# A two-layer encoder on one core: another order for the first stage's loads and products, and half a projection moved ahead of the second pair's gates

## The chip, the cores and the metric

The kernel runs on one core of a Trainium2 chip. The metric is the device time of one execution in microseconds. Engines are named as the profile names them: PE multiplies matrices (PEld loads its weights), DVE, ACT and POOL work on vectors, SP issues the DMAs.

## The reference

A hybrid encoder with two layers, 1024 tokens of 1024 channels, in float32. Cut to what matters:

```python
def even_mixer(h, ...):                       # layer 0
    q, k, v, g_a, x_b, g_b = split(h @ w_in)
    a_out = diff_attention(q, k, v, ...)      # 4 heads, two softmax maps each, RMS norm per head
    xc = depthwise_conv(x_b, conv_w) + conv_b
    gate_a, gate_x = sigmoid(xc @ w_a + b_a), sigmoid(xc @ w_x + b_x)   # per direction
    log_a = -LRU_C * gate_a * softplus(-lam)
    u = sqrt(-expm1(2 * log_a)) * gate_x * xc
    b_out = scan(exp(log_a), u) + reverse_scan(exp(log_a), u)
    return concat(a_out * silu(g_a), b_out * silu(g_b)) @ w_out

def odd_mixer(h, ...):                        # layer 1: 16 heads over an 8 x 16 window
    q, k, v, g = split(h @ w_in)
    return (neighborhood_attention(q, k, v, rpb) * silu(g)) @ w_out

for l in range(2):
    shift, scale, gate = split(silu(c) @ ada_w[l] + ada_b[l])
    h = rms_norm(x, norm_g[l]) * (1 + scale) + shift
    x = x + gate * (even_mixer, odd_mixer)[l](h)
return rms_norm(x, final_g)
```

## The kernel before

Everything is kept transposed, channels on the partitions, tokens along the row, in two halves of 512 tokens (half 0 and half 1). A weight slab is 128 output columns of a weight matrix. To keep float32 accuracy each operand is split into a high and a low part: ACT writes a slab's high part (`whi`, L189), POOL its low part in four pieces (`wlo`, L192), and each 128x128 by 128x512 product is three matmuls: high by high, low activations, low weights (L208 to L210, and L577 to L579 in the first stage). A projection of one slab for one half is eight products, 24 matmuls into one PSUM bank. The activations' parts are `ahi` (ACT, L419) and `alo` (DVE, L420).

A scheduler places instructions by priority, in the order of the code; `tc.issue_after(x)` holds what follows behind x, `tc.high_priority()` lets it go ahead. Each engine then runs its instructions in that fixed order, and so do the DMA queues, which SP fills in the order in which it issues.

**The first stage** (L517 to L624) loads x in 16 pieces `xT` and squares them (`sq`), sums the squares over the channels on PE (`norm`), makes 1/sqrt on DVE by Newton steps (`rstd_rows`, L385), and spreads it back with PE (`spread`). `mod_first(g)` loads eight pieces of the modulation's weights (`ada`), sums on PE (`mod`, 32 small matmuls) and gives the scale and shift of channel blocks 2g and 2g+1. `parts(g, hf)` scales those blocks of a half into `ahi` and `alo`, and `products(i, g, hf)` multiplies them with slab i of the first three. Slabs 0 and 1 hold x_b, from which the convolution starts (ACT L715, DVE L723, then the parts `xch` and `xcl` for the gates).

**The recurrent part.** A list of jobs sets PE's order: projections, and `pair(c, c+1)`, which makes the gates (`gate`) of two channel blocks, then their exponentials and square roots on ACT (table loads between), then the input factors (L795), the two scans (L798, L800) and their sum (L802) on DVE. The names of the projections are `gb` (the branch gate g_b, whose PSUM bank is read last by DVE at L681, `sgb`), `v3` (the fourth block of v), and `k0`, `q0` (keys and queries of head 0). There are four PSUM banks for projections, given out in turn: `k0` of half 1 takes the bank that `gb2` of half 1 has left, and can't start before DVE's L681 on it.

**The layer boundary.** The last block of layer 0's output is added to x (DVE L1153), squared (ACT L1158), added to the running sum (DVE L1164) and summed on PE (`ssl`). Behind it PE starts layer 1's projections.

**rstd_rows** is called twice in the first stage, for eight head norms in layer 0's attention (`osq`, then `obc` on PE and `vT` on DVE), and at the boundary.

Of the kernel before, what the change touches and what calls it, by code (L numbers as in the profile page):

```python
# [15 lines left out]
ALU = mybir.AluOpType  # L16
# [81 lines left out]
def kernel(ctx, tc, xT, xTp, small, lamp, adaw, tb, w0, gw, wo0, w1, nab, wo1, out):  # L98
# [53 lines left out]
    def load_next():  # L152
        i = state["load"]
        if i >= len(slabs):
            state["load"] = i + 1
            return
        raws[i] = wp.tile([P, KC, P], F32, tag="raw", name=f"raw{i}")
        nc.sync.dma_start(raws[i][:], slabs[i])
        state["load"] = i + 1

    def split_next():
        i = state["split"]
        if i >= len(slabs):
# [20 lines left out]
        hi = pool.tile([P, KC, P], F32R, tag=tags[0], name=f"whi{i}")  # L184
        lo = pool.tile([P, KC, P], F32R, tag=tags[1], name=f"wlo{i}")

        with (tc.issue_after(state["tanh"]) if i == at1["k", 1] else nullcontext()), (
                tc.high_priority() if j < 2 else tc.issue_after(state["pool"])):
            A.activation(hi[:], raw[:], AF.Copy)  # L189

            for k in range(0, KC, 2):
                G.tensor_tensor(lo[:, k:k + 2], raw[:, k:k + 2], hi[:, k:k + 2], ALU.subtract)  # L192
        ready[i] = (hi, lo)
        state["split"] = i + 1
        while state["load"] <= i + state["depth"]:
            load_next()
# [80 lines left out]

    def mod_first(g, pool, small, c32):

        ps = ptp.tile([P, HF], F32, tag="pt", name=f"mod{g}")  # L280

        def sums(x, w, start, stop):
# [6 lines left out]
        for k in range(KC):  # L289
# [4 lines left out]
            src = adaw[0, k * P:(k + 1) * P, :2 * D].rearrange("p (t n) -> p t n", t=2)  # L294
            state["ada"] = nc.sync.dma_start(piece[:], src[:, :, 2 * g * P:(2 * g + 2) * P])
            pieces.append(piece)
        if g == 0:
            for k in range(KC):
                sums(pieces[k], c32[:, k, :], k == 0, k == KC - 1)
# [85 lines left out]
    def rstd_rows(ss, n, pool, spare=None, add=EPS):  # L385


        if spare is not None:
            v, rr, t = (spare[:, i * P:(i + 1) * P] for i in range(3))
        else:  # L390
            v, rr, t = (pool.tile([P, P], F32, tag=g, name=g)[:] for g in ("rs", "rr", "rt"))
        V.tensor_scalar(v, ss[:, :P], 1.0 / n, add, ALU.mult, ALU.add)
        V.tensor_scalar(rr.bitcast(I32), v.bitcast(I32), -0.5, float(0x5F3759DF),
                        ALU.mult, ALU.add)
        for _ in range(3):
            V.scalar_tensor_tensor(t, rr, -0.5, rr, ALU.mult, ALU.mult)
            V.tensor_tensor(t, t, v, ALU.mult)
            V.scalar_tensor_tensor(rr, t, 1.5, rr, ALU.add, ALU.mult)
        return rr

    def rstd_rows_act(ss, n, pool, w):
# [6 lines left out]

    def spread(rr, bc, w=P):
        for j in range(4):  # L410
            T.matmul(bc[:, j * w:(j + 1) * w], state["sel"][:, j, :], rr[:, :w], start=True, stop=True)

    def make_h(l, k, hf, x, bc):

# [17 lines left out]
    def evac_v(h):  # L432
# [3 lines left out]
            A.activation(mixed[h][:, hf * HF:(hf + 1) * HF], ps[:], AF.Copy)  # L436
        return f


    c_q, c_k, c_v, c_g, c_xb, c_gb = 0, 4, 8, 12, 16, 20  # L440
    order0 = [c_xb, c_xb + 1, c_v, c_xb + 2, c_xb + 3, c_v + 1, c_v + 2, c_gb, c_gb + 1]
    order0 += [c_v + 3, c_gb + 2, c_gb + 3, c_k, c_q]
    for h in range(1, DA_HEADS):
        order0 += [c_k + h, c_q + h]
    order0 += [c_g]
# [71 lines left out]
    with tc.tile_pool(name="start", bufs=2) as stp, tc.tile_pool(name="ada0", bufs=KC) as adp:  # L517
# [12 lines left out]
        def squares(hf, on_dve, pool, tag):  # L530
# [5 lines left out]
            for k in range(KC):  # L536
# [8 lines left out]
            if hf:  # L545
                ss_add(ss, sqs[KC - 1], True, False)
                with tc.issue_after(state["ssmm"].ins):
                    for k in range(KC - 1):
                        ss_add(ss, sqs[k], False, k == KC - 2)
# [17 lines left out]
        def products(i, g, hf):  # L567
# [7 lines left out]
            for k in (2 * g, 2 * g + 1):  # L575
                ps, (wh, wl), (hi, lo) = banks[i, hf], ready[i], hact[k, hf]
                T.matmul(ps, wh[:, k, :], hi[:], start=k == 0, stop=False)  # L577
                T.matmul(ps, wl[:, k, :], hi[:], start=False, stop=False)
                T.matmul(ps, wh[:, k, :], lo[:], start=False, stop=k == KC - 1)  # L579

        squares(0, (2, 5), pp, "pp")
        mod_first(0, adp, stp, c32)
        slab(0)
        scale(0)
        parts(0, 0)
        with tc.issue_after(state["ada"].ins):
            squares(1, (1, 4, 7), ptp, "pt")
        slab(1)
        with tc.issue_after(state["x"].ins):
            mod_first(1, adp, stp, c32)  # L590
        products(0, 0, 0)
        products(1, 0, 0)
        slab(2)
        with tc.issue_after(state["modmm"].ins):
            scale(1)
        parts(0, 1)
        with tc.issue_after(state["x"].ins):
            mod_first(2, adp, stp, c32)
        for i in range(2):
            products(i, 0, 1)  # L600

        rest = [(2, 0, 0), (2, 0, 1)]
        for g in range(1, KC // 2):
            if g == 1:
                with tc.issue_after(state["x"].ins):
                    mod_first(3, adp, stp, c32)
# [5 lines left out]
            for args in rest:  # L612
                products(*args)
            rest = [(2, g, 0), (2, g, 1)]
        for i, evac in enumerate((evac_xb(0), evac_xb(1))):
            for hf in range(2):
                evac(hf, banks[i, hf])
# [73 lines left out]
    def some(gen, n):  # L691
        for _ in range(n):
            next(gen, None)

    def after_dve(gen, n):

# [8 lines left out]
    with tc.tile_pool(name="lru", bufs=1) as lp:  # L705
# [178 lines left out]
        def mod_step():  # L884
            for m in parts_:
# [244 lines left out]
    def out_layer(l, ato, xsrc, xdst, pool, korder, order, view, segments):  # L1130
# [5 lines left out]
        def run(s):  # L1136
# [11 lines left out]
            for c in range(KC):  # L1148
                load(c + 1)

                def evac(hf_, ps, c=c):
# [463 lines left out]
```

## Time and profile before

| | |
|---|---|
| median of 3 runs | 1177.58 us (1175.38 to 1177.91) |
| profiled execution | 1177.39 us |
| its span | 1175.70 us (1.69 us lie outside it) |
| PE busy | 1141.5 us, 97% of the span |
| DVE, ACT, POOL busy | 715.5, 561.6, 442.4 us |

The span begins with the first instruction of the profile and all positions below are microseconds from there. A matmul's end is modelled: rows of 128x512 matmuls that follow each other start 0.23 us apart while each is given 0.39 us, so an idle time of PE in a row is 0.16 us shorter than what the wait really took from the next start.

### The profile page before, as it was taken

The page shows a single profiled execution, that of the slowest core. Times are in us where ns is not written, and L with a number is a line of the kernel's source. Part 1 is how long each engine was busy: PE and PEld are TensorE (multiplying, and loading weights), DVE is VectorE, ACT ScalarE, POOL GpSimd, SP SyncE. Part 2 cuts the span into 40 slices and gives each one's busy share as a digit, 9 for nine tenths or more (in the row PEclk, how much of TensorE's full clock was granted, in tenths as well). Part 3 has the DMA queues.
Part 4 walks back from the last instruction along what each step waited for, and adds up shares of the span by engine and source line. Part 5 has one row for each costly group of instructions (what it writes and reads, how often), then busy time and mean ns, then how long its engine had stood idle before and what let it go on. Part 6 is the DMA issues. An engine that isn't in the chain of part 4 may idle for free.

```text
span 1175.7 us, 19488 instructions
## 1 busy us (share of the span) xinstructions
PE 1141.5 (97%) x7232; PEld 972.5 (83%) x7232; DVE 715.5 (61%) x1420; ACT 561.6 (48%) x1032; POOL 442.4 (38%) x588
## 2 busy tenths in 40 slices
PE   5999999999999999999999999999999999999996
PEld 3788778888887888778879889988988998888896
DVE  6857968699899989768472434234444443454353
ACT  4357685476555556433343444344444444355221
POOL 3135445243333332466533433333243333417200
PEclk9999999999999999999999999999999999999998
DMA  9723141422122112485513533243453543314312
GB/s 330 241 71 118 54 141 54 143 85 80 32 82 79 32 38 73 144 301 183 179 60 117 153 104 101 87 141 113 119 160 98 156 147 96 95 35 154 101 73 72
DMA packets 85727, 136.48 MB, mean 116 GB/s; under 512 B 7936, under 2 KB 49408, under 8 KB 85632
## 3 DMA queue, kind: packets, MB, share of 16 engines
q1 hardware_dynamic: 85632, 135.23, 36.7%
q8 instruction: 57, 0.93, 0.3%
q14 instruction: 38, 0.31, 0.1%
HBM read 112.13 MB, written 16.78 MB: 110 GB/s over the span
## 4 chain that ended last, share of the span: by engine, by line
PE 79%; DVE 10%; ACT 5%; DMA 2%; POOL 2%; issue 1%; SPq 0%; DVEq 0%; ACTq 0%; POOLq 0%
PE pp L208 15%; PE pp L209 15%; PE pp L210 15%; PE no L1423 4%; PE etr L1405 3%; PE v L208 3%; PE v L210 3%; PE v L209 3%; PE n L675 2%; PE atr L1037 2%; DVE e L1007 2%; PE n L676 2%; POOL wlo L192 2%; PE s L675 2%; PE s L676 1%; DMA raw<-in_wo_dram 1%
## 5 line engine op out<-in xcount | busy, mean ns | idle before, releaser
L208 PE MATMUL pp<-ahi,whi 128*128 128x512 f32 (+1 forms) x976 | 370.0, 379 | 0.1
L209 PE MATMUL pp<-alo,whi 128*128 128x512 f32 (+1 forms) x976 | 368.1, 377 | 0.0
L210 PE MATMUL pp<-ahi,wlo 128*128 128x512 f32 (+1 forms) x976 | 367.6, 377 | 0.2 <-POOL wlo L192 0.2
L192 POOL TENSOR_TENSOR wlo<-raw,whi 128x256 fp32r<-128x256 f32 x320 | 265.6, 862 | 219.5 <-ACT whi L189 199.0
L210 PEld LDWEIGHTS pp<-ahi,wlo 128*128 128x128 f32 x976 | 183.8, 188 | 34.4 <-POOL wlo L192 0.6
L208 PEld LDWEIGHTS pp<-ahi,whi 128*128 128x128 f32 x976 | 183.8, 188 | 32.5 <-issue 1.1
L209 PEld LDWEIGHTS pp<-alo,whi 128*128 128x128 f32 x976 | 183.9, 188 | 30.6 <-issue 0.2
L1394 POOL TENSOR_SCALAR e<-e,r 128x288 f32<-128x288 f32 (+1 forms) x128 | 71.5, 572 | 221.0 <-DVE r L1392 215.7
L189 ACT ACTIVATE whi<-raw 128x1024 fp32r<-128x1024 f32 x80 | 84.4, 1057 | 106.2 <-PE pp L209 58.7
L1011 ACT ACTIVATE e<-e,nm 128x1024 f32<-128x1024 f32 x64 | 73.7, 1151 | 46.5 <-DVE nm L1007 46.2
L1389 ACT ACTIVATE e<-e,nm 128x288 f32<-128x288 f32 (+1 forms) x128 | 72.8, 570 | 46.4 <-DVE nm L1386 45.9
L1386 DVE CUSTOM_DVE_ANT_0 e<-n,bias 128x288 f32<-128x288 f32 (+1 forms) x128 | 60.6, 504 | 49.4 <-PE n L676 32.0
L1411 DVE COPY e<-etr 96x384 f32<-96x384 f32 (+1 forms) x64 | 35.5, 554 | 89.1 <-PE etr L1405 88.8
L1409 ACT ACTIVATE e<-etr 96x384 f32<-96x384 f32 (+1 forms) x64 | 31.4, 490 | 115.8 <-DVE e L1411 113.3
L1007 DVE CUSTOM_DVE_ANT_0 e<-s,tb 128x1024 f32<-128x1024 f32 x64 | 77.3, 1219 | 5.8 <-PE s L676 4.9
L1028 POOL TENSOR_SCALAR e<-e,r 128x256 f32<-128x256 f32 x32 | 32.7, 1021 | 124.4 <-DVE r L1017 75.7
L208 PE MATMUL v<-whi,ahi 128*128 128x256 f32 x256 | 72.2, 282 | 0.0
L210 PE MATMUL v<-whi,alo 128*128 128x256 f32 x256 | 71.9, 281 | 0.0
L209 PE MATMUL v<-wlo,ahi 128*128 128x256 f32 x256 | 71.9, 281 | 0.0
L1044 ACT ACTIVATE ath<-atr 128x512 fp32r<-128x512 f32 x64 | 37.5, 597 | 37.5 <-PE atr L1037 37.3
L1153 DVE SCALAR_TENSOR_TENSOR xh<-pp,mod,xh 128x512 f32<-128x512 f32 (+1 forms) x37 | 23.4, 633 | 50.5 <-PE pp L210 46.1
L1405 PE MATMUL etr<-ident,e 128*96 128x128 f32 (+1 forms) x384 | 52.3, 272 | 0.8 <-POOL e L1394 0.8
(222 smaller groups left out, 2118.4 us busy)
## 6 DMA issues: line engine op xcount, KB each, us to landing
raw<-in_w_dram SPq DMA_DIRECT2D x56, 512.0 KB
ada<-in_adaw_dram SPq DMA_DIRECT2D x96, 256.0 KB
raw<-in_wo_dram SPq DMA_DIRECT2D x24, 512.0 KB
bias<-in_nab_dram SPq DMA_DIRECT2D x64, 144.0 KB
qq<-qq SPq DMA_DIRECT2D x48, 128.0 KB
bias<-in_nab_dram SPq DMA_DIRECT2D x32, 192.0 KB
xT<-in_xT_dram SPq DMA_DIRECT2D x16, 256.0 KB
vd<-vt SPq DMA_DIRECT2D x32, 128.0 KB
```

What stands on the lines that cost most here:

```text
L189: A.activation(hi[:], raw[:], AF.Copy)
L192: G.tensor_tensor(lo[:, k:k + 2], raw[:, k:k + 2], hi[:, k:k + 2], ALU.subtract)
L208: T.matmul(ps, lh, rh, start=start, stop=False)
L209: T.matmul(ps, lh, rl, start=False, stop=False)
L210: state["pe"] = T.matmul(ps, ll, rh, start=False, stop=stop).ins
L675: T.matmul(dst, qsel(q[m]), k, start=True, stop=False)
L1007: state["dve"] = V.tensor_tensor_reduce(out=e[:], in0=ps[:].rearrange("p a b -> p (a b)"), in1=tbt["tb"][:, o:o + S], scale=-1.0, scalar=3 ...
L1011: A.activation(e[:], e[:], AF.Exp, scale=-1.0, bias=nm[:], accum_out=sums[:, m:m + 1])
L1386: state["dve"] = V.tensor_tensor_reduce(out=e[:, m, :n], in0=ps[:, m, :n], in1=bias["now"][m][:, :n], scale=-1.0, scalar=3.0e38, op0=ALU.a ...
L1389: A.activation(e[:, m, :n], e[:, m, :n], AF.Exp, scale=-1.0, bias=nm[:, m:m + 1], accum_out=sums[:, m:m + 1])
L1394: state["pool"] = G.tensor_scalar(e[:, m, :n], e[:, m, :n], r[:, m:m + 1], 0.0, ALU.mult, ALU.add).ins
L1405: T.transpose(pt[:kn, m, j * P:(j + 1) * P], e[:, m, j * kn:(j + 1) * kn], ident[:])
```

## The change

Four edits. The first stage loads the third slab and the second group of modulation weights ahead of the second half of x, and PE's products are written in another order: two groups of half 0 for all three slabs, then the sums of half 1, then its first two groups, then the rest. Half 0 of `v3` stands ahead of the second pair's gates, half 1 behind them. At the layer boundary, the split of the gate slab of layer 1 waits for the last square. `rstd_rows` has seven instructions behind the first guess, where it had nine.

```diff
     def split_next():
...
-        with (tc.issue_after(state["tanh"]) if i == at1["k", 1] else nullcontext()), (
+        behind = {at1["g", 0]: "sq", at1["k", 1]: "tanh"}.get(i)
+        with (tc.issue_after(state[behind]) if behind else nullcontext()), (
                 tc.high_priority() if j < 2 else tc.issue_after(state["pool"])):
             A.activation(hi[:], raw[:], AF.Copy)
...
     def rstd_rows(ss, n, pool, spare=None, add=EPS):
...
-        for _ in range(3):
-            V.scalar_tensor_tensor(t, rr, -0.5, rr, ALU.mult, ALU.mult)
-            V.tensor_tensor(t, t, v, ALU.mult)
-            V.scalar_tensor_tensor(rr, t, 1.5, rr, ALU.add, ALU.mult)
+        c = 0.375
+        V.scalar_tensor_tensor(t, rr, 1.0, rr, ALU.mult, ALU.mult)
+        V.tensor_tensor(t, t, v, ALU.mult)
+        V.scalar_tensor_tensor(t, t, -10.0 / 3.0, t, ALU.add, ALU.mult)
+        V.scalar_tensor_tensor(rr, t, 5.0, rr, ALU.add, ALU.mult)
+        V.scalar_tensor_tensor(t, rr, -0.5 * c ** 3, rr, ALU.mult, ALU.mult)
+        V.tensor_tensor(t, t, v, ALU.mult)
+        V.scalar_tensor_tensor(rr, t, 1.5 * c, rr, ALU.add, ALU.mult)
...
-    order0 = [c_xb, c_xb + 1, c_v, c_xb + 2, c_xb + 3, c_v + 1, c_v + 2, c_gb, c_gb + 1]
-    order0 += [c_v + 3, c_gb + 2, c_gb + 3, c_k, c_q]
+    order0 = [c_xb, c_xb + 1, c_v, c_xb + 2, c_xb + 3, c_v + 1, c_v + 2, c_gb, c_v + 3]
+    order0 += [c_gb + 1, c_gb + 2, c_gb + 3, c_k, c_q]
...
         slab(0)
         scale(0)
         parts(0, 0)
+        slab(1)
+        with tc.issue_after(state["raw"]):
+            next(first_mods[1])
         with tc.issue_after(state["ada"].ins):
-            squares(1, (1, 4, 7), ptp, "pt")
-        slab(1)
+            second = squares(1, (1, 4, 7), ptp, "pt")
...
         products(0, 0, 0)
         products(1, 0, 0)
-        slab(2)
+        next(first_mods[1])
         with tc.issue_after(state["modmm"].ins):
+            products(2, 0, 0)
+        parts(1, 0)
+        products(0, 1, 0)
+        with tc.issue_after(state["pe"]):
+            sums_in_a_run(*second)
+        with tc.issue_after(state["ssmm"].ins):
+            products(1, 1, 0)
+            products(2, 1, 0)
+        with tc.issue_after(state["pe"]):
             scale(1)
-        parts(0, 1)
...
+        for g in range(2):
+            parts(g, 1)
+            for i in range(3):
+                products(i, g, 1)
+        next(first_mods[3])
+        for g in range(2, KC // 2):
...
-                six_banks(weave(pair((2, 3)), gb(1), first_ys((1, 0)), turns=(2, 1, 1))),
-                vj(3), gb(2), gb(3), kq0(), proj(at0[c_k + 1], 0, evac_k(("a", 1)))]
+                proj(at0[c_v + 3], 0, evac_v(3)),
+                six_banks(weave(pair((2, 3)), gb(1), first_ys((1, 0)), turns=(2, 1, 1))),
+                proj(at0[c_v + 3], 1, evac_v(3), prep=False), gb(2), gb(3), kq0(), proj(at0[c_k + 1], 0, evac_k(("a", 1)))]
...
-                    A.activation(sq[:, :n], x, AF.Square)
+                    state["sq"] = A.activation(sq[:, :n], x, AF.Square).ins
```

On SP, in the first stage behind the first eight pieces of `ada`, a raw slab and the x of half 0. Before:

```order
L532 DMA xT_116<-in_xT_dram 128x512
L532 DMA xT_117<-in_xT_dram 128x512
L532 DMA xT_118<-in_xT_dram 128x512
L532 DMA xT_119<-in_xT_dram 128x512
L532 DMA xT_120<-in_xT_dram 128x512
L532 DMA xT_121<-in_xT_dram 128x512
L532 DMA xT_122<-in_xT_dram 128x512
L532 DMA xT_123<-in_xT_dram 128x512
L158 DMA raw_398<-in_w_dram 128x1024
L295 DMA ada<-in_adaw_dram 128x2x256 x8
L158 DMA raw_477<-in_w_dram 128x1024
L295 DMA ada<-in_adaw_dram 128x2x256 x16
```

The same place now (`raw_339` is the third slab, `raw_398` before):

```order
L158 DMA raw_339<-in_w_dram 128x1024
L298 DMA ada<-in_adaw_dram 128x2x256 x8
L547 DMA xT_116<-in_xT_dram 128x512
L547 DMA xT_117<-in_xT_dram 128x512
L547 DMA xT_118<-in_xT_dram 128x512
L547 DMA xT_119<-in_xT_dram 128x512
L547 DMA xT_120<-in_xT_dram 128x512
L547 DMA xT_121<-in_xT_dram 128x512
L547 DMA xT_122<-in_xT_dram 128x512
L547 DMA xT_123<-in_xT_dram 128x512
L298 DMA ada<-in_adaw_dram 128x2x256 x16
L158 DMA raw_424<-in_w_dram 128x1024
```

The x of half 1 moved behind one slab and eight pieces of `ada`, which moved ahead of its eight pieces.

On PE, where the second pair's gates begin (`pp_1_...` is the bank of a projection's half 1, `pp_0_...` of half 0; `gwh` and `gwl` are the gate weights' parts). Before, the gates follow `gb0` of half 1 directly:

```order
L208 MATMUL pp_1_1405<-ahi_1_762,whi_1327 128x512
L209 MATMUL pp_1_1405<-alo_1_763,whi_1327 128x512
L210 MATMUL pp_1_1405<-ahi_1_762,wlo_1328 128x512
L208 MATMUL gate<-xch_1209,gwh_1052 128x512
L209 MATMUL gate<-xcl_1210,gwh_1052 128x512
L210 MATMUL gate<-xch_1209,gwl_1053 128x512
```

Now the first product of `v3` stands there:

```order
L210 MATMUL pp_1_1401<-ahi_1_770,whi_1323 128x512
L211 MATMUL pp_1_1401<-alo_1_771,whi_1323 128x512
L212 MATMUL pp_1_1401<-ahi_1_770,wlo_1324 128x512
L210 MATMUL pp_0_1431<-ahi_0_322,whi_1392 128x512
L211 MATMUL pp_0_1431<-alo_0_323,whi_1392 128x512
L212 MATMUL pp_0_1431<-ahi_0_322,wlo_1393 128x512
```

24 matmuls of `v3` half 0 come first, then the gates. Between the gates' end and `k0` of half 1 there are now six projections (`v3` half 1, `gb2` and `gb3`, `k0` half 0), where there were seven.

On ACT at the layer boundary; `sq<-xh_1_7` is the last square, `raw_5767` the gate slab, `raw_5728` the slab of q0. Before:

```order
L189 ACTIVATE whi_5760<-raw_5677 128x1024
L1158 ACTIVATE sq<-xh_1_6_5638 128x512
L189 ACTIVATE whi_5828<-raw_5767 128x1024
L189 ACTIVATE whi_5769<-raw_5728 128x1024
L1158 ACTIVATE sq<-xh_1_7_5689 128x512
```

Now, where the gate slab is `raw_5745` and that of q0 `raw_5706`:

```order
L191 ACTIVATE whi_5738<-raw_5655 128x1024
L1192 ACTIVATE sq<-xh_1_6_5616 128x512
L191 ACTIVATE whi_5747<-raw_5706 128x1024
L1192 ACTIVATE sq<-xh_1_7_5667 128x512
L191 ACTIVATE whi_5804<-raw_5745 128x1024
```

The gate slab's split moved from in front of the other split and the square to behind both.

## Rows read from the trace of the kernel before

**Rows 1.** Waits of PE: us in total, times, longest us.

```profile
PE obc L411 <- DVE osq L398: 1.3, 2, 0.7
...
PE gate L208 <- DVE sgb L681: 0.9, 1, 0.9
...
PE gate L210 <- POOL gwl L744: 0.6, 1, 0.6
```

**Rows 2.** Windows: busy us (count) of PE, PEld, DVE, ACT, POOL; PEclk, DMA, GB/s.

```profile
24.00:26.00 2.00, 1.57 (x5) 0.83 (x5) 2.00 (x3) 1.59 (x4) 2.00 (x3) 0.76 1.05 369
26.00:28.00 2.00, 2.00 (x6) 1.57 (x6) 2.00 (x2) 2.00 (x5) 1.63 (x2) 0.50 1.10 352
28.00:30.00 2.00, 1.77 (x25) 1.19 (x27) 1.38 (x3) 1.07 (x2) 0.86 (x2) 0.89 1.10 348
...
40.00:42.00 2.00, 2.00 (x30) 1.24 (x32) 2.00 (x4) 0.40 (x1) 0.00 (x0) 0.50 1.11 349
```

**Rows 3.** Timeline of PE, first stage: start, us, instruction [idle before, releaser].

```profile
24.43 0.50 PE L577 MATMUL start<-ahi,whi 128*128 128x512 f32 x1 [1.99 <-ACT ahi L419]
...
29.43 1.95 PE L382 MATMUL norm<-sq,ones 128*32 128x128 f32 x64 [0.23 <-DVE sq L539]
...
38.40 0.58 PE L577 MATMUL start<-ahi,whi 128*128 128x512 f32 x1 [1.99 <-ACT ahi L419]
...
73.38 0.39 PE L208 MATMUL pp<-ahi,whi 128*128 128x512 f32 x1
```

**Rows 4.** Timeline of DVE, the convolution of the first pair.

```profile
68.32 8.21 DVE L723 SCALAR_TENSOR_TENSOR xc<-xb,sm,xc 128x1022 f32<-128x1022 f32 x5 [9.66 <-ACT xc L715]
76.46 1.82 DVE L733 TENSOR_TENSOR xcl<-xc,xch 128x512 fp32r<-128x512 f32 x2
```

**Rows 5.** Timeline of PE: first matmuls of v3 and of k0's half 1.

```profile
164.73 0.39 PE L208 MATMUL pp<-ahi,whi 128*128 128x512 f32 x1
...
203.01 0.39 PE L208 MATMUL pp<-ahi,whi 128*128 128x512 f32 x1
```

**Rows 6.** Timeline of DVE behind the second pair's gates.

```profile
181.64 1.23 DVE L795 SCALAR_TENSOR_TENSOR t<-t,w 128x1024 f32<-128x1024 f32 x1 [1.68 <-ACT w L791]
182.90 2.29 DVE L798 TENSOR_TENSOR_SCAN t<-t,t 128x1024 f32<-128x1024 f32 x1
...
188.21 2.83 DVE L800 TENSOR_TENSOR_SCAN w<-t,t 128x1024 f32<-128x1024 f32 x1
...
195.25 1.76 DVE L795 SCALAR_TENSOR_TENSOR t<-t,w 128x1024 f32<-128x1024 f32 x1
...
201.94 0.68 DVE L681 SCALAR_TENSOR_TENSOR sgb<-sgb,pp 128x512 f32<-128x512 f32 x1
...
206.07 0.68 DVE L681 SCALAR_TENSOR_TENSOR sgb<-sgb,pp 128x512 f32<-128x512 f32 x1
```

**Rows 7.** Timeline of POOL there.

```profile
176.98 2.84 POOL L192 TENSOR_TENSOR wlo<-raw,whi 128x256 fp32r<-128x256 f32 x4 [6.96 <-ACT whi L189]
187.87 8.05 POOL L192 TENSOR_TENSOR wlo<-raw,whi 128x256 fp32r<-128x256 f32 x4 [8.05 <-ACT whi L189]
199.89 5.48 POOL L192 TENSOR_TENSOR wlo<-raw,whi 128x256 fp32r<-128x256 f32 x4 [3.97 <-ACT whi L189]
```

**Rows 8.** One line's view, of L397: op, count, ns min/median/max, first and last start.

```profile
L397 DVE TENSOR_TENSOR osq<-osq x24: 281/292/551, 269.3 to 495.3; 128x128 f32<-128x128 f32 x24
```

**Rows 9.** Timelines of ACT, DVE and PE at the layer boundary.

```profile
584.44 2.01 ACT L189 ACTIVATE whi<-raw 128x1024 fp32r<-128x1024 f32 x2 [6.30 <-DMA raw<-in_w_dram]
586.35 0.62 ACT L1158 ACTIVATE sq<-xh 128x512 f32<-128x512 f32 x1
...
582.09 0.75 DVE L1153 SCALAR_TENSOR_TENSOR xh<-pp,mod,xh 128x512 f32<-128x512 f32 x1 [3.10 <-PE pp L210]
...
588.30 0.43 PE L382 MATMUL ssl<-sq,ones 128*32 128x128 f32 x8 [0.81 <-DVE sq L1164]
589.58 0.50 PE L210 MATMUL pp<-ahi,wlo 128*128 128x512 f32 x1 [0.19 <-POOL wlo L192]
```

More of the change, by code (lines that the diff above doesn't have):

```diff
@@ L157, in load_next @@
         raws[i] = wp.tile([P, KC, P], F32, tag="raw", name=f"raw{i}")
-        nc.sync.dma_start(raws[i][:], slabs[i])
+        state["raw"] = nc.sync.dma_start(raws[i][:], slabs[i]).ins
         state["load"] = i + 1
@@ L296, in mod_first @@
             pieces.append(piece)
+        yield
         if g == 0:
@@ L319, in mod_first @@
             first_mod[2 * g + j] = gain[:, j:j + 1], m[:, 0, j:j + 1]
+        yield
     def mod_part(l, t, part, pool, tag="ada", bufs=2, acc=None, wait=3, apart=False,
@@ L410, in spread @@
         for j in range(4):
-            T.matmul(bc[:, j * w:(j + 1) * w], state["sel"][:, j, :], rr[:, :w], start=True, stop=True)
+            state["spread"] = T.matmul(bc[:, j * w:(j + 1) * w], state["sel"][:, j, :], rr[:, :w], start=True,
+                                       stop=True).ins
     def make_h(l, k, hf, x, bc):
@@ L437, in evac_v, with some @@
         return f
+    def some(gen, n):
+        for _ in range(n):
+            next(gen, None)
     c_q, c_k, c_v, c_g, c_xb, c_gb = 0, 4, 8, 12, 16, 20
-    order0 = [c_xb, c_xb + 1, c_v, c_xb + 2, c_xb + 3, c_v + 1, c_v + 2, c_gb, c_gb + 1]
-    order0 += [c_v + 3, c_gb + 2, c_gb + 3, c_k, c_q]
+    order0 = [c_xb, c_xb + 1, c_v, c_xb + 2, c_xb + 3, c_v + 1, c_v + 2, c_gb, c_v + 3]
+    order0 += [c_gb + 1, c_gb + 2, c_gb + 3, c_k, c_q]
     for h in range(1, DA_HEADS):
@@ L544, in squares, with sums_in_a_run @@
                     ss_add(ss, sq, k == 0, k == KC - 1)
[L545 to L549, printed above, removed]
+            return ss, sqs
+        def sums_in_a_run(ss, sqs):
+            ss_add(ss, sqs[KC - 1], True, False)
+            with tc.issue_after(state["ssmm"].ins):
+                for k in range(KC - 1):
+                    ss_add(ss, sqs[k], False, k == KC - 2)
         bcs = {}
@@ L578, in products @@
                 T.matmul(ps, wl[:, k, :], hi[:], start=False, stop=False)
-                T.matmul(ps, wh[:, k, :], lo[:], start=False, stop=k == KC - 1)
+                state["pe"] = T.matmul(ps, wh[:, k, :], lo[:], start=False, stop=k == KC - 1).ins
         squares(0, (2, 5), pp, "pp")
-        mod_first(0, adp, stp, c32)
+        first_mods = [mod_first(g, adp, stp, c32) for g in range(KC // 2)]
+        some(first_mods[0], 2)
         slab(0)
@@ L585 @@
         parts(0, 0)
+        slab(1)
+        with tc.issue_after(state["raw"]):
+            next(first_mods[1])
         with tc.issue_after(state["ada"].ins):
-            squares(1, (1, 4, 7), ptp, "pt")
-        slab(1)
+            second = squares(1, (1, 4, 7), ptp, "pt")
+        state["depth"] = 0
+        slab(2)
         with tc.issue_after(state["x"].ins):
-            mod_first(1, adp, stp, c32)
+            next(first_mods[2])
+        with tc.issue_after(state["ada"].ins):
+            next(first_mods[3])
+        with tc.issue_after(state["ada"].ins):
+            load_next()
         products(0, 0, 0)
         products(1, 0, 0)
-        slab(2)
+        next(first_mods[1])
         with tc.issue_after(state["modmm"].ins):
-            scale(1)
-        parts(0, 1)
[L597 to L606, printed above, removed]
+            products(2, 0, 0)
[3 more added lines that the diff above has]
+            sums_in_a_run(*second)
+        with tc.issue_after(state["ssmm"].ins):
+            products(1, 1, 0)
+            products(2, 1, 0)
+        with tc.issue_after(state["pe"]):
+            scale(1)
+        with tc.issue_after(state["spread"]):
+            next(first_mods[2])
+        for g in range(2):
+            parts(g, 1)
+            for i in range(3):
+                products(i, g, 1)
+        next(first_mods[3])
+        for g in range(2, KC // 2):
             for hf in range(2):
@@ L611 @@
                     products(i, g, hf)
-            for args in rest:
-                products(*args)
             rest = [(2, g, 0), (2, g, 1)]
+            if g < KC // 2 - 1:
+                for args in rest:
+                    products(*args)
         for i, evac in enumerate((evac_xb(0), evac_xb(1))):
@@ L689, in mods @@
             yield from mod_part(*later_mods.popleft(), pool, **kw)
-    def some(gen, n):
-        for _ in range(n):
-            next(gen, None)
     def after_dve(gen, n):
```

## The prediction

> **What bounds the kernel now.** The page's first part comes first: PE is busy 97% of the span, every other engine 61% or less. So the kernel ends when PE has done its work, and an edit is worth only what it takes from, or adds to, PE's idle time and PE's slow time. The view of PE's waits shows where idle time lies that this change touches: two waits before a head norm's spread, and two at the second pair's gates [rows 1]. The timeline of PE adds the first stage (two waits of 1.99 us for `ahi`) and the layer boundary (0.81 and 0.19 us) [rows 3, 9]. The windows show the slow time. Behind the first of the 1.99 us waits the granted clock is 0.76, 0.50 and 0.89 in three windows of 2 us, the lower of the two levels (1.2 GHz where 2.4 is full): 0.48 + 1.00 + 0.22 = 1.7 us lost. The second wait is followed by 0.50 as well [rows 2]. Elsewhere PE has work in its queue, so what I ask of each edit is whether PE then waits, and how long, since a wait of about 2 us is paid nearly twice.
>
> **First stage.** The loads: one slab (512 KB) and eight pieces of `ada` (2 MB) pass the x of half 1, and at the 348 to 369 GB/s of these windows [rows 2] that is 7 us later for the x of half 1 and 2.1 MB, 6 us, earlier for the second group's weights. Removed: PE no longer runs out of work at 38.40, because group 1 of half 0 and the third slab's products stand ahead of half 1. That wait (1.99, and 0.16 that the modelled end hides) and its slow stretch (1.7) go: -3.85. Added: the sums of half 1 (1.95 us on PE, [rows 3]) now come behind a last square whose x lands 7 us later; DVE's queue has that square in front of `alo` of group 1, so PE waits for it. I put this at 1.45, from 7 us of delay less the 5.5 us (24 matmuls at 0.227) of products that were moved ahead. So the stage should end 2.4 us before its 73.38. Not all of it reaches the end. The first gates need `xcl`, whose chain runs from the last product of slab 0 over a convolution of 8.21 us on DVE; `xcl` begins at 76.46 and its first half is there 0.91 us later, at 77.4 [rows 4]. Slab 0 is not done earlier (by my count of the matmuls in front, 0.3 us later), while PE comes to the gates 24 matmuls behind the stage, at 73.38 - 2.4 + 5.44 = 76.4. It then waits 1.2 us or so. Net: **-1.2**, between -2.4 (no such wait) and 0.
>
> **Second pair of gates.** Removed: with 5.44 us more work in front, the bank that DVE frees and the weights that POOL splits are there when the gates come. Two waits go, 0.9 and 0.6 [rows 1], each 0.16 longer than shown: -1.8. But this half projection is taken from behind the gates. `k0` of half 1 starts 203.01 - 164.73 = 38.28 us behind the gates' end, which is exactly seven projections [rows 5], and its bank comes free at 201.94 + 0.68 = 202.62 [rows 6]: a slack of 0.4 us. Now six projections stand there, 38.28 x 6/7 = 32.8 us. What frees the bank is a chain that starts with the last gate: sigmoid, exponentials and roots on ACT, then DVE without a gap of note from 181.64. It took 202.62 - 164.73 = 37.9 us. It gets shorter by the L681 on `gb2` half 0 (0.68), which is issued ahead of the scans now: 37.2. So PE has at least 37.2 + 0.1 - 32.8 = 4.5 us of nothing to do, queued behind one matmul.
>
> How long exactly hangs on POOL. Four pieces of a split take 2.84 us when DVE is quiet and 8.05 us beside the scans [rows 7], and the scan beside them takes 2.83 where another takes 2.29, an L795 1.76 where another takes 1.23 [rows 6]: each pays. Before, q0's split began at 199.89, with DVE's chain nearly done. Splits follow PE's release of a slab, so with one projection fewer both fall 5.4 us earlier against DVE: k0's on the first scan and the two L795 behind it, q0's on the second reverse scan. Three to four instructions more at 0.53 each, less one that is spared, is +1.6 by these rows if they overlap wholly; I take 1.3, and 0 to 2.1 as bounds. Then PE waits 38.5 + 0.1 - 32.8 = 5.8 us, less the 1.8 that went: **+4.0** (2.7 to 4.8). A wait of 5.8 us is longer than the two that were followed by half clock, so I add one more such stretch, **+1.7** (0 to 1.7).
>
> The page "SBUF — State Buffer" of the Trainium skill says in its section "Who interferes with whom" that a DVE instruction with two SBUF inputs contends with a GpSimd instruction that reads SBUF. By it all of the scans and L795 under a split would be slowed, and the sum would hold the 1.6 rather than 1.3; without it, 0. The trace agrees with it by the 8.05 against 2.84.
>
> **rstd_rows.** Two instructions of 0.292 us (0.33 from start to start) go from each call [rows 8]: 0.65. In the first stage and at the boundary PE has products in front meanwhile; this costs and gives nothing. In the attention both waits of PE for `osq` (0.7 and 0.6) [rows 1] hang on the chain's last instruction. Each gets 0.65 shorter: **-1.3** (0 if other DVE work stands in between, -2 if later waits shrink too).
>
> **Layer boundary.** ACT waited for the gate slab's DMA until 584.44, then made two splits, and the last square came at 586.35; its input was ready at 582.84 [rows 9]. With the gate slab behind, ACT does q0's split and then the square, both before 584.5; DVE's addition follows, and PE comes to the sums at 587.3 with them ready. The 0.81 + 0.16 go, and of the 0.19 + 0.16 before L210, for which POOL had the gate slab's four pieces in front of q0's, all: **-1.3** (-0.9 to -1.4). The gate slab's split is later by two instructions; PE has q0's and k's projections in front of it.
>
> **Sum.** -1.2 + 4.0 + 1.7 - 1.3 - 1.3 = +1.9. The profiled execution took 1177.39 us, so 1179.3; the median of the runs shown is 0.2 higher, so 1179.5. I take **1179.3**. A difference under 0.2% (2.4 us) can't be told from none here, so this is "no change", close to its upper edge. Its own range is 1177 to 1181.5.
>
> **Rivals.**
> *A, the bank is not what PE waits for.* If the chain behind the gates follows its own backlog (DVE was late from the first pair) and not the last gate, it starts no later than before, k0 finds its bank free, and the four gains stand alone: -1.2 - 1.8 - 1.3 - 1.3 = -5.6, 1172.0. For it: the gates' own waits were for DVE, so DVE was behind there. Against it: DVE itself waited 1.68 us for ACT at 181.64 [rows 6], and ACT's exponentials stand behind the last sigmoid.
> *B, slower: the next bank is late too.* Behind the freed bank, DVE frees that of `gb3` half 0 after 206.07 - 201.94 = 4.13 us [rows 6]; `q0` half 0 needs it one projection (5.47) after k0's. With PE held, k0 half 0's two additions (0.68 each by the nearest row, an estimate) get in front: 5.5, and already nothing is left. Four instructions slowed by 0.53 under the next split would make PE wait 2 us once more and lose another 1.7 to the clock: +3.7, 1183.1. It decides once that interval passes 5.5 us. Against it: those splits need PE's release, and PE is late.
> *C, a cheaper wait.* The splits don't touch DVE's chain and the clock stays up: +2.7 in place of +5.7, so -1.1, 1176.3. For it: before, q0's split began only at 199.89 [rows 7]. Against: both long waits in these rows brought the clock down.
> *D, the first stage gives all or nothing* (-2.4 or 0): it moves the sum by 1.2 and stays inside the forecast's range.
>
> **Chances.** Forecast 0.42 (of this 0.25 within 0.2%, 0.17 slower), A 0.17 (faster 0.16), B 0.19 (slower), C 0.22 (0.17 within, 0.05 faster). Together: faster 0.21, same 0.43, slower 0.36. The range leaves out most of A (0.13) and the upper part of B (0.07): 1173.5 to 1183.2.
>
> **What would show it.** In the changed profile PE's longest wait should stand before the first matmul of `k0` half 1, 5 to 6.5 us long, released by DVE's `sgb` at about 205 to 207, with windows at a clock of 0.5 behind it and POOL's splits of 6 us or more on both sides. No wait should be left at the second gates, before `ssl`, or at 38 us; one of about 1 us should stand at the first gates. If the first products of `k0` half 1 start without a wait, A is right and I am wrong by 7 us; a second wait one projection later is B. If waits for `osq` remain as long as before, the two instructions were not on the path.

## The result, and the profile after

The changed kernel takes 1180.95 us (median of 7 runs, 1179.9 to 1181.29), the kernel before in the same runs 1176.75. The ratio is 1.003 with a 95% interval of 1.0020 to 1.0041: 2.4 to 4.8 us slower. The forecast was 1179.3, no change at its upper edge, with a range of 1173.5 to 1183.2.

The profiled execution took 1181.29 us, its span 1179.6. Seven places of PE's timeline tell where the 3.9 us between the two spans lie (start of the row named, in us from the span's start; the last column is what the stretch since the line above added):

| place | before | after | later by | added |
|---|---|---|---|---|
| first pp matmul (end of the first stage) | 73.38 | 72.97 | -0.41 | -0.41 |
| first gate matmul on `xcl` | 79.04 | 80.03 | 0.99 | +1.40 |
| `k0` half 1 | 203.01 | 208.38 | 5.37 | +4.38 |
| first logits of the attention | 224.77 | 231.86 | 7.09 | +1.72 |
| boundary sums `ssl` | 588.30 | 591.80 | 3.50 | -3.59 |
| last `ssl` | 1166.16 | 1169.36 | 3.20 | -0.30 |
| end of span | 1175.70 | 1179.60 | 3.90 | +0.70 |

The view of PE's waits after the change, its longest rows without those of the first 15 us:

```profile
PE pp L210 <- DVE sgb L718: 5.7, 1, 5.7
PE start L594 <- ACT ahi L430: 3.4, 3, 2.0
...
PE gate L211 <- DVE xcl L766: 1.2, 1, 1.2
```

The two waits at the second gates [rows 1] are gone, and one of 5.7 us has come. PE's timeline after the change, at the rows that answer to [rows 3], at the first gate on `xcl`, at `k0` half 1 [rows 5] and at the boundary [rows 9]:

```profile
23.95 0.73 PE L594 MATMUL start<-ahi,whi 128*128 128x512 f32 x1 [1.99 <-ACT ahi L430]
...
31.74 0.39 PE L314 MATMUL mod<-pick,mrow 128*128 128x4 f32 x2 [0.64 <-ACT mrow L312]
...
34.22 0.76 PE L594 MATMUL start<-ahi,whi 128*128 128x512 f32 x1 [1.06 <-ACT ahi L430]
...
72.97 0.39 PE L210 MATMUL pp<-ahi,whi 128*128 128x512 f32 x1
...
80.03 0.50 PE L211 MATMUL gate<-xcl,gwh 128*128 128x512 f32 x1 [1.24 <-DVE xcl L766]
...
208.38 0.80 PE L210 MATMUL pp<-ahi,whi 128*128 128x512 f32 x1 [5.73 <-DVE sgb L718]
...
591.80 0.43 PE L387 MATMUL ssl<-sq,ones 128*32 128x128 f32 x8
```

The wait at 38.40 of before became one of 0.64 at 31.74 and one of 1.06 at 34.22, `k0` half 1 waits 5.73 for DVE's `sgb`, and `ssl` waits no more. The windows (PEclk is the third number from the end) show what followed the wait at 34.22 and what lies around the one of `k0`:

```profile
34.00:36.00 2.00, 1.78 (x4) 1.09 (x5) 1.89 (x3) 0.78 (x2) 0.00 (x0) 0.57 1.10 351
36.00:38.00 2.00, 2.00 (x24) 1.23 (x26) 0.00 (x0) 0.00 (x0) 0.00 (x0) 0.58 1.10 349
...
204.00:206.00 2.00, 0.00 (x0) 0.00 (x0) 2.00 (x1) 1.46 (x3) 0.32 (x1) 0.74 0.38 137
206.00:208.00 2.00, 0.00 (x0) 0.00 (x0) 1.97 (x3) 0.00 (x0) 0.00 (x0) 0.50 0.73 252
208.00:210.00 2.00, 1.62 (x4) 1.33 (x5) 1.97 (x3) 0.00 (x0) 0.00 (x0) 0.50 0.11 43
210.00:212.00 2.00, 2.00 (x7) 1.58 (x6) 1.92 (x4) 1.23 (x2) 0.00 (x0) 0.56 0.39 147
```

The clock is down behind both, 0.50 to 0.58, near the lower of its two levels (1.2 of 2.4 GHz). At `k0` it falls while PE still waits, and PE pays for the part in which it has work again: 1.7 us. DVE's timeline behind the gates (answers to [rows 6]) and POOL's [rows 7]:

```profile
188.02 2.71 DVE L831 TENSOR_TENSOR_SCAN t<-t,t 128x1024 f32<-128x1024 f32 x1
190.66 3.37 DVE L828 SCALAR_TENSOR_TENSOR t<-t,w 128x1024 f32<-128x1024 f32 x2
193.95 2.82 DVE L833 TENSOR_TENSOR_SCAN w<-t,t 128x1024 f32<-128x1024 f32 x1
196.69 2.26 DVE L831 TENSOR_TENSOR_SCAN t<-t,t 128x1024 f32<-128x1024 f32 x1
198.88 1.69 DVE L835 TENSOR_TENSOR t<-t,w 128x1024 f32<-128x1024 f32 x1
200.50 1.75 DVE L828 SCALAR_TENSOR_TENSOR t<-t,w 128x1024 f32<-128x1024 f32 x1
...
203.65 2.82 DVE L833 TENSOR_TENSOR_SCAN w<-t,t 128x1024 f32<-128x1024 f32 x1
...
207.65 0.68 DVE L718 SCALAR_TENSOR_TENSOR sgb<-sgb,pp 128x512 f32<-128x512 f32 x1
```

```profile
187.76 6.87 POOL L194 TENSOR_TENSOR wlo<-raw,whi 128x256 fp32r<-128x256 f32 x4 [8.17 <-ACT whi L191]
198.21 6.11 POOL L194 TENSOR_TENSOR wlo<-raw,whi 128x256 fp32r<-128x256 f32 x4 [3.59 <-ACT whi L191]
```

Both splits now lie beside DVE's chain. Of the rows up to 203.65 only the scan at 196.69, between the splits, has its undisturbed length.

### The profile page after: what moved, and what is told of

Same layout as the page of the kernel before. It is cut to its first block, busy times and chain, and to the rows that moved or that the text cites. A ratio compares the mean times of both kernels' runs of the same rounds, so it can differ in the third digit from the quotient of the medians.

```text
span 1179.6 us, 19460 instructions
## 1 busy us (share of the span) xinstructions
PE 1143.3 (97%) x7232; PEld 974.5 (83%) x7232; DVE 707.1 (60%) x1396; ACT 558.9 (47%) x1030; POOL 441.8 (37%) x588
## 4 chain that ended last, share of the span: by engine, by line
PE 82%; DVE 9%; DMA 3%; ACT 2%; issue 2%; POOL 1%; SPq 0%; DVEq 0%; ACTq 0%; POOLq 0%
PE pp L210 17%; PE pp L211 17%; PE pp L212 17%; PE no L1457 4%; PE etr L1439 3%; PE v L210 3%; PE v L212 3%; PE v L211 3%; DVE e L1041 2%; PE n L712 2%; PE atr L1071 2%; PE n L713 2%; PE s L712 1%; PE s L713 1%; DMA ada<-in_adaw_dram 1%
## 5 line engine op out<-in xcount | busy, mean ns | idle before, releaser
L353 DVE SCALAR_TENSOR_TENSOR macc<-ada,ctmp,macc 128x512 f32<-128x512 f32 x56 | 48.1, 859 | 9.2 <-DMA ada<-in_adaw_dram 9.0
L712 PE MATMUL s<-ks,qq 128*128 128x512 f32 x128 | 52.8, 412 | 0.7 <-DVE nm L1041 0.7
```

The source lines that it names most:

```text
L353: V.scalar_tensor_tensor(acc[:], piece[:], ctmp[:, k:k + 1], acc[:], ALU.mult, ALU.add)
L712: T.matmul(dst, qsel(q[m]), k, start=True, stop=False)
```

## The experiments

Each ratio is to the kernel before, run on the same chip.

**1. The pair's edit alone.**

```diff
-    order0 = [..., c_gb, c_gb + 1]
-    order0 += [c_v + 3, c_gb + 2, ...]
+    order0 = [..., c_gb, c_v + 3]
+    order0 += [c_gb + 1, c_gb + 2, ...]
...
+                proj(at0[c_v + 3], 0, evac_v(3)),
                 six_banks(weave(pair((2, 3)), gb(1), ...)),
-                vj(3), gb(2), gb(3), ...
+                proj(at0[c_v + 3], 1, evac_v(3), prep=False), gb(2), gb(3), ...
```

> The kernel before with the second pair's edit alone: half 0 of v3 ahead of the gates and one projection fewer behind them. Theory (bank): the first matmul of k0 half 1 waits 5 to 6.5 us for DVE's sgb and half clock follows; with the two gate waits that go, +4.2 and +1.7, so 1182 to 1183.5 us against 1176.8 of before. Rival (first stage): the wait is there only because the first stage made the chain behind the gates late; alone the edit costs under 2 us, under 1179.

Ratio 1.0065 (1.0052 to 1.0078), +7.7 us. The wait is the same to the hundredth with the pair's edit alone:

```profile
207.58 0.79 PE L208 MATMUL pp<-ahi,whi 128*128 128x512 f32 x1 [5.73 <-DVE sgb L681]
```

So the rival falls. The cost is above what was expected: in this profile the clock falls later in the wait and more of the slow stretch meets work, 2.7 us from `k0` half 1 to the logits where the changed kernel lost 1.7.

**2. The first stage's edit alone**: `squares`, `sums_in_a_run`, `mod_first` as a generator, and the order of the products, as in the diff above; `order0`, `jobs`, `rstd_rows` and the boundary as before.

```diff
         products(0, 0, 0)
         products(1, 0, 0)
-        slab(2)
+        next(first_mods[1])
...
```

> The kernel before with the first stage's edit alone. Theory (second slow stretch): PE still waits about 1 us near 34 us, the clock falls there as before, the stage ends within 0.5 us of before, the first gates wait 1.2 us for xcl: +0.5 to +1.7 us, 1177.3 to 1178.5. Rival (as forecast): the edit is worth -1.2, 1175.5, and the loss seen in the whole comes from elsewhere.

Ratio 1.0010 (1.0001 to 1.0019), +1.2 us, as expected. The prediction's -1.2 is out. Its profile has the wait (1.09 us, at 34.11), a clock of 0.67 and 0.50 in the windows behind, and 1.24 us of waiting at the first gate on `xcl`.

**3. The shorter rstd_rows and the boundary's edit, without the rest**: these two hunks on the kernel before.

```diff
-        for _ in range(3):
...
+        V.scalar_tensor_tensor(rr, t, 1.5 * c, rr, ALU.add, ALU.mult)
...
+        behind = {at1["g", 0]: "sq", at1["k", 1]: "tanh"}.get(i)
```

> The kernel before with the shorter rstd_rows and the boundary's edit alone. Theory (waits in the attention): -1.3 at the boundary and -2.6 in the attention, 1172.5 to 1173.5. Rival (phase): part of the attention's gain came from the shifted start of the attention and not from rstd_rows; then -2.6 in all, about 1174.2.

Ratio 0.9969 (0.9957 to 0.9981), -3.7 us (-5.1 to -2.2), median 1173.94: in front of both kernels. That lies between the theory and the rival, and the interval holds both -3.9 and -2.6.

**4. The changed kernel without the pair's edit** (the reverse of the diff of 1).

```diff
-    order0 = [..., c_gb, c_v + 3]
-    order0 += [c_gb + 1, c_gb + 2, ...]
+    order0 = [..., c_gb, c_gb + 1]
+    order0 += [c_v + 3, c_gb + 2, ...]
...
-                proj(at0[c_v + 3], 0, evac_v(3)),
...
```

> The changed kernel without the second pair's edit. Theory (the parts add): the changed kernel less 5.9 us, 1174.5 to 1175.5. Rival: with the first stage's later chain the second pair's gates lose more than before even without the edit, 1176.5 or more.

Ratio 0.9975 (0.996 to 0.999), -2.9 us, median 1173.67, a little below the range expected: the pair's edit costs the whole 0.55%, 6.5 us. This profile also has the first stage's wait, and yet no slow stretch behind it:

```profile
33.75 0.50 PE L594 MATMUL start<-ahi,whi 128*128 128x512 f32 x1 [0.96 <-ACT ahi L430]
...
78.66 0.50 PE L211 MATMUL gate<-xcl,gwh 128*128 128x512 f32 x1 [1.24 <-DVE xcl L766]
```

```profile
34.00:36.00 2.00, 1.56 (x6) 0.72 (x5) 1.53 (x3) 0.37 (x1) 0.00 (x0) 1.00 1.08 348
36.00:38.00 2.00, 2.00 (x66) 1.75 (x65) 0.00 (x0) 0.00 (x0) 0.00 (x0) 1.00 1.10 348
```

With the clock up the first gate comes at 78.66, 1.4 us before that of the changed kernel's profile.

**5. The wait filled.** In the changed kernel, `k0` half 0 is computed twice into its bank.

```diff
...
-        kq0 = lambda: chain(both(at0[c_k], evac_k(("a", 0))), ...
+        kq0 = lambda: chain(proj(at0[c_k], 0, evac_k(("a", 0)), times=2),
+                            proj(at0[c_k], 1, evac_k(("a", 0))), ...
```

> The changed kernel, with the product k0 half 0 computed twice into the same bank (24 matmuls, 5.4 us of added work, result unchanged), which lies where PE waits for the bank of k0 half 1. Theory (the wait itself is not the whole price; the clock falls in it): the wait shrinks from 5.7 to under 0.5 us, k0 half 1 starts at the same time, the clock stays at full, and the kernel gets 1.5 to 2.7 us faster in spite of 5.4 us more work: 1178.3 to 1179.5 against 1181.0. Rival (the clock falls there anyway or the bank comes later still): 1181 to 1183.

Ratio 1.0015 (1.0007 to 1.0024), median 1179.48: by the ratios 1.8 us (0.15%) less than the changed kernel, with 24 matmuls more. The two intervals overlap a little (1.0020 to 1.0024), so the size is uncertain.

```profile
207.79 0.50 PE L210 MATMUL pp<-ahi,whi 128*128 128x512 f32 x1 [0.38 <-DVE sgb L718]
```

```profile
206.00:208.00 2.00, 1.62 (x8) 1.04 (x7) 2.00 (x3) 0.00 (x0) 0.00 (x0) 1.00 0.59 197
208.00:210.00 2.00, 2.00 (x10) 1.62 (x10) 1.57 (x2) 0.36 (x1) 0.00 (x0) 1.00 0.35 131
```

Counted from the last gate matmul, `k0` half 1 starts no earlier (39.3 us behind it, 39.2 in the changed kernel), but at full clock, and from there to the first logits PE takes 21.90 us, in the changed kernel 23.48. So the slow stretch is a cost of its own, and it went when PE's idling was filled.

**6. POOL kept off the last scan.** In the changed kernel, POOL's split of q0 first copies one column of the last scan's output, so it waits for it.

```diff
+            if i == at0[c_q]:
+                G.tensor_copy(lo[:, 0, 0:1], state["scan"][:, 0:1])
             for k in range(0, KC, 2):
                 G.tensor_tensor(lo[:, k:k + 2], raw[:, k:k + 2], hi[:, k:k + 2], ALU.subtract)
...
                     V.tensor_tensor(mixed[4 + c][:], mixed[4 + c][:], w[:], ALU.add)
+                    state["scan"] = w
```

> The changed kernel, with POOL's split of q0's weights made to wait for the last scan (one 128x1 copy on POOL reads the scan's output first). Theory (DVE and POOL hold each other up): L835, L828, L848 and the last L833 take 1.2, 1.2, 1.3 and 2.3 us in place of 1.69, 1.75, 1.56 and 2.82, the bank comes 1.8 us earlier, PE's wait is 3.9 us: 1179.0 to 1179.6. Rival (the scans are slow for another reason): durations and time as in the changed kernel, 1181.0.

DVE's rows are as the theory has them, and so is the wait of `k0` half 1 (3.82 us); but a second wait comes two projections later:

```profile
198.37 1.20 DVE L837 TENSOR_TENSOR t<-t,w 128x1024 f32<-128x1024 f32 x1
199.49 1.21 DVE L830 SCALAR_TENSOR_TENSOR t<-t,w 128x1024 f32<-128x1024 f32 x1
...
201.77 2.29 DVE L835 TENSOR_TENSOR_SCAN w<-t,t 128x1024 f32<-128x1024 f32 x1
```

```profile
205.97 0.80 PE L212 MATMUL pp<-ahi,whi 128*128 128x512 f32 x1 [3.82 <-DVE sgb L720]
...
216.16 0.50 PE L212 MATMUL pp<-ahi,whi 128*128 128x512 f32 x1 [2.11 <-DVE sgb L720]
```

SP's timeline of this kernel says why: the load of the next raw slab waits for the split to free its buffer, and `y`'s store, ready at 206.7, stands behind it in SP's queue.

```profile
209.55 0.33 SPq L158 DMA_DIRECT2D raw<-in_w_dram  x1
209.97 0.38 SPq L864 DMA_DIRECT2D yd<-y  x1
```

ACT then waits 5.9 us for that store to free the buffer of the next `sgb`. Ratio 1.0039 (1.0027 to 1.0051), median 1182.74 where 1179.0 to 1179.6 was expected: the contention is shown, but no time is won.

**7. The first stage's wait filled**: the kernel of 2, with six matmuls whose result nothing reads.

```diff
             products(2, 0, 0)
+            for n in range(2):
+                (wh, wl), (hi, lo) = ready[2], hact[n % 2, 0]
+                T.matmul(banks[2, 1], wh[:, n % 2, :], hi[:], start=n == 0, stop=False)
...
         parts(1, 0)
```

> The kernel with the first stage's edit alone, and six matmuls whose result nothing reads ahead of group 1 of half 0, where PE waits 1.1 us for ahi. Theory (this wait is what brings the second slow stretch): the wait is under 0.3 us, the clock stays at full from 28 us on, the stage ends 1.4 to 2.0 us earlier than with the edit alone: 1176.1 to 1176.7 against 1178.1. Rival (the sums of half 1 and the last square set the pace, or the clock falls all the same): no gain, 1178 or more.

Ratio 1.0000 (0.9992 to 1.0009) against 1.0010 without the filling: the right direction, but the intervals overlap, and the rival (no gain) is not excluded. In its profile this wait for `ahi` is gone and the clock is 1.00 from 28 us on, but in that of experiment 4 it is 1.00 from 29 us on without filling. Since the fall doesn't come in each execution, one profile can't show that the filling kept it away.

**8. k0 ahead of gb2 and gb3**, in the changed kernel.

```diff
-    order0 += [c_gb + 1, c_gb + 2, c_gb + 3, c_k, c_q]
+    order0 += [c_gb + 1, c_k, c_gb + 2, c_gb + 3, c_q]
...
-                proj(at0[c_v + 3], 1, ...), gb(2), gb(3), kq0(), ...
+                proj(at0[c_v + 3], 1, ...), both(at0[c_k], ...), gb(2), gb(3), both(at0[c_q], ...), ...
```

> The changed kernel with k0 ahead of gb2 and gb3, in the order of slabs and of jobs, so that the projections whose banks are freed behind the scans start 11 us later. Theory (bank): the user of gb2 half 1's bank is now the ninth projection behind the gates, 43.7 us, and the chain takes 40.3 at most: no wait there, no wait at the gates: 1172 to 1174. Rival (the wait only moves, to gb3 on the banks of k0, whose evacuation stands among the scans): 1177 or more.

Ratio 1.0012 (1.0004 to 1.0021), median 1179.15, between the two kernels and not the 1172 to 1174 of the theory. No projection waits, neither `k0` nor `gb3`; the first logits wait for the parts of q0 instead, which stand behind the last `y` on ACT, DVE and SP:

```profile
227.56 0.77 PE L712 MATMUL s<-ks,qq 128*128 128x512 f32 x1 [4.44 <-DMA qq<-qq]
```

Behind that wait the clock is 0.50 again (228 to 232 us).

**9. Six banks in turn for the projections behind the gates**, in the changed kernel; PE's order stays.

```diff
-                proj(at0[c_v + 3], 1, ...), gb(2), gb(3), kq0(), proj(at0[c_k + 1], 0, ...)]
+                from_first(six_banks(chain(proj(at0[c_v + 3], 1, ...), gb(2), gb(3), kq0(),
+                                           proj(at0[c_k + 1], 0, ...))))]
```

> The changed kernel with six PSUM banks in turn, from v3 half 1 on, for the projections behind the second pair's gates, where it has four: k0 half 1 gets the bank of v3 half 1, which ACT frees early, and gb2 half 1's bank goes to q0 half 1, 43.7 us behind the gates. PE's order is unchanged. Theory (only the bank holds k0 half 1): no wait there and no fall of the clock, 7.5 us less: 1173 to 1174. Rival (the whole chain of g_b is late by then: q0's parts come behind it on ACT and DVE): the first logits wait 3 to 5 us for q0 and the clock falls there, 1177 to 1179.

Ratio 0.9991 (0.9982 to 1.0000), median 1177.26: 3.9 parts in a thousand (4.6 us) less than the changed kernel, where the theory gave 7.5. `k0` half 1 doesn't wait; the logits do, and the clock behind them is 0.50 (228 to 230 us), as the rival had it:

```profile
227.50 0.76 PE L712 MATMUL s<-ks,qq 128*128 128x512 f32 x1 [3.34 <-DVE ql L700]
```

The bank was the first thing that made PE wait for the late chain, and q0's parts, behind that same chain on DVE, are the next.

**10. The same six banks with the old first stage**: the edit of 9, with the pair's edit, the shorter rstd_rows and the boundary's edit, on the kernel before. Against 9:

```diff
-        first_mods = [mod_first(g, adp, stp, c32) for g in range(KC // 2)]
-        some(first_mods[0], 2)
+        mod_first(0, adp, stp, c32)
...
-        with tc.issue_after(state["ada"].ins):
-            second = squares(1, (1, 4, 7), ptp, "pt")
+        with tc.issue_after(state["ada"].ins):
+            squares(1, (1, 4, 7), ptp, "pt")
...
```

> The same six banks on the kernel before with the other three edits (half of v3 ahead of the gates, rstd_rows, the boundary), the first stage as before. Theory: 0.5 to 1.5 us less than with the new first stage. Rival (the first stage's edit gives as forecast): 1 us more.

Ratio 0.9992 (0.9983 to 1.0000), in 9 it is 0.9991: no difference between the two first stages here, where 0.5 to 1.5 us was expected.

**11. The shorter rstd_rows alone**, on the kernel before.

```diff
-        for _ in range(3):
-            V.scalar_tensor_tensor(t, rr, -0.5, rr, ALU.mult, ALU.mult)
...
+        c = 0.375
+        V.scalar_tensor_tensor(t, rr, 1.0, rr, ALU.mult, ALU.mult)
...
```

> The kernel before with the shorter rstd_rows alone. Theory (two waits for osq, and the waits behind them that hang on the same chain: vT, the head's transposes, the modulation row near 525 us): -2.3 to -2.7, 1175.0 to 1175.5 against 1177.6. Rival (as forecast: two waits of 0.65): -1.3, 1176.3.

Ratio 0.9990 (0.9981 to 0.9998), -1.2 us; the interval doesn't tell -1.3 from -2.3. In its profile PE takes 1.9 us less from the first logits to `ssl`. The first wait for `osq` [rows 1] shrinks from 0.72 to 0.36 and the other is gone:

```profile
375.60 1.16 PE L415 MATMUL obc<-osq,sel 128*128 128x128 f32 x8 [0.36 <-DVE osq L402]
```

**12. The boundary's edit alone**, on the kernel before.

```diff
-        with (tc.issue_after(state["tanh"]) if i == at1["k", 1] else nullcontext()), (
+        behind = {at1["g", 0]: "sq", at1["k", 1]: "tanh"}.get(i)
+        with (tc.issue_after(state[behind]) if behind else nullcontext()), (
...
-                    A.activation(sq[:, :n], x, AF.Square)
+                    state["sq"] = A.activation(sq[:, :n], x, AF.Square).ins
```

> The kernel before with the boundary's edit alone. Theory: -1.3, with PE going from the last product to the sums without a wait. Rival (part of the gain is given back where the gate slab is used first): -0.5 or less.

Ratio 0.9987 (0.9978 to 0.9996), -1.5 us: as expected.

## Why the prediction was right, and where it was not

**The pair's edit: right, in mechanism and size.** Forecast +4.0 and +1.7; the table's stretches have 4.38 and 1.72, and without the edit the kernel is 6.5 us faster (4). The chain from the gates' end to the freed bank was put at 38.5 us, PE's wait at 5.8: the wait is 5.73. That DVE pays for POOL's splits is shown by 6: the four instructions that lie beside the second split in the changed kernel lie before it there, and fall back to 1.20, 1.21, 1.24 and 2.29. The Trainium skill's page "SBUF — State Buffer", section "Who interferes with whom", which names DVE instructions with two SBUF inputs and a GpSimd instruction that reads SBUF, agrees: L835 takes 1.69 under a split and 1.20 without. The slow clock as a price apart is shown by 5. Rival A is out by the wait itself, B since no second projection waits in the changed kernel, and C since both the splits and the clock cost what was forecast. What the prediction did not see is how deep the cause lies: 8 and 9 take the wait for the bank away and get back only part, because everything behind the gates is about 5.4 us later against PE, q0's parts included.

**The first stage: wrong.** Two steps failed. The first is the 1.45 of plain idling that I put in place of the wait and its slow stretch (-3.85). I had DVE's last square hold up `alo`; in this profile PE doesn't wait for `alo` (in five others with this stage 0.27 to 0.44), but for ACT, in two places. At 31.74 it waits 0.64 for `mrow`, which ACT makes 1.0 us after the sums' end at 30.44, behind squares of the later x:

```profile
30.16 1.36 ACT L556 ACTIVATE sq<-xT 128x512 f32<-128x512 f32 x2 [0.65 <-DMA xT<-in_xT_dram]
31.43 0.26 ACT L312 ACTIVATE mrow<-mod 128x128 f32<-128x128 f32 x1
```

At 34.22 it waits 1.06 for `ahi`: from the `mod` matmul to the first product on the new `ahi` it is 2.5 us (before 2.3, 36.12 to 38.40), and the new order leaves PE four matmuls for that time. Behind it the clock is 0.57 and 0.58 in two windows, 1.7 us lost, so no slow stretch was saved in that execution. The stage ended 0.4 us earlier, not 2.4.

The second step is "Slab 0 is not done earlier (by my count of the matmuls in front, 0.3 us later)". ACT's first `xb` of slab 0 starts at 66.37, before at 64.06: 2.3 us later. The wait at the first gates, 1.24 us, came as forecast, but the net there was +1.0 against -1.2, also outside both cases of D. The clock is not the whole of this: in the profile of 4, which has no second slow stretch, the stage ends 1.8 us earlier than before, and the first gate on `xcl` only 0.4.

A single profile says little here, since a slow stretch (1.7 us each) comes in one execution and not in another, with either first stage. The kept profiles together, without that of 7 (slow stretches up to 46 us, and means in us from the span's start; "first `xb`" is the first time that ACT reads slab 0's sums, "stage end" the first `pp` matmul):

| first stage | slow stretches | first `xb` | stage end | first gate on `xcl` |
|---|---|---|---|---|
| old (before, 1, 3, 10, 11, 12) | 2, 2, 3, 3, 2, 1 | 64.6 | 74.0 | 79.6 |
| new (changed, 2, 4, 5, 6, 8, 9) | 2, 2, 1, 1, 2, 1, 0 | 65.8 | 72.4 | 79.5 |

So on the mean of these few profiles the new order does save about one slow stretch and 1.5 us at the stage's end, but slab 0 is 1.2 us later and holds the gates, and nothing is left. The times agree: +1.2 (0.1 to 2.2) alone (2), 0.7 by the ratios of 4 and 3, within their intervals, and none by 9 against 10.

What decides about a slow stretch stays open. In each of the seven new profiles PE waits 0.96 to 1.09 us for that `ahi`; the clock falls behind it in three (the changed kernel, 2, 6), in four not. Nor did it fall behind the wait of 1.99 us in 12 (PE's timeline and the window there):

```profile
38.37 0.50 PE L578 MATMUL start<-ahi,whi 128*128 128x512 f32 x1 [1.99 <-ACT ahi L420]
```

```profile
38.00:40.00 2.00, 1.62 (x5) 0.78 (x5) 2.00 (x4) 1.65 (x3) 0.00 (x0) 1.00 1.08 351
```

So the 1.7 that the prediction took off for the wait at 38.40 was not certain to be there either. The Trainium skill's page "TensorE: Matmul & The Clock Gate", section "What's actually happening", lets the moment of a change of clock depend on a phase that does not restart with the kernel. That would fit a fall that comes in one execution and not in another; no run here shows that it is the reason.

**rstd_rows: right in the places, the size open.** Forecast -1.3; the time alone gave -1.2 (-2.2 to -0.2), the profile of 11 -1.9, and the changed kernel's -3.59 up to the boundary leaves -2.6 when the boundary's 0.97 is taken off. Of both, about 0.9 (0.71 and the hidden 0.16) is a wait near 525 us behind a slab's DMA that is also absent in 12, without the edit: not its doing. That leaves -1.0 and -1.7. Of the two waits for `osq` the first got 0.36 shorter, not 0.65, and the second (0.57 and the hidden 0.16) went.

**The boundary: right.** Forecast -1.3; 0.97 before `ssl` and 0.30 behind it in the table, -1.5 in time (12).

**The sum.** +1.9 was forecast, +3.5 (2.4 to 4.8) measured: inside the forecast's own range, but slower, where "no change" was said. The first stage's term explains 2.2 of the profile's difference, the attention gives 1.3 of it back, and 0.7 at the span's end is the last spread at half clock, which the profile of 11 has too. That the sum came near is in part luck, since the first two pull against each other. The parts measured alone (+7.7, +1.2, -1.2, -1.5: +6.2) are 2.7 more than the whole; 1.0 of that is the longer slow stretch in the profile of the pair's edit alone, and the rest can't be told from the noise of four intervals of 1 us or more to either side.

## What to carry to other kernels

Work moved ahead of the start of a long chain delays everything that hangs on the chain by its length, and the slack at the chain's end is what pays: read that slack (0.4 us here) before moving, and look not only at the first thing that waits but at the next ones. A wait of TensorE of 1 to 2 us was followed by a slow stretch of 1.7 us in some executions and not in others, so count that stretch as a range, also where an edit is to take it away. When work is reordered, follow the product that the next stage waits for, and not only the end of the stage. Of the four edits two were worth having: with rstd_rows and the boundary alone the kernel takes 1173.9 us, ratio 0.9969.

## What the runs showed of the hardware that was not expected

With 24 matmuls added in a wait of 5.7 us the clock stayed up, PE took 1.6 us less from `k0` half 1 to the logits (5), and the kernel's time was less, not more. The same wait of about 1 us in the same place was followed by half clock in three profiles and not in four, and a wait of 1.99 us by full clock in 12. And with a POOL split moved out of DVE's way, a store whose input was ready at 206.7 was issued at 209.97, because the load that the split lets go stands ahead of the store in SP's queue (6).
